# A two-layer mixer and mixture-of-experts backbone: the output projection in two parts, and expert products on tiles of 32 columns

## The chip, the cores and the metric

The kernel runs on one core of one Trainium2 chip. The time is the device time of one execution in microseconds. Before the change it is 1985.58 us in the median of three runs (1981.42 to 1986.17). One further execution was profiled: 1986.72 us, of which the profile's span, from the first instruction to the last, is 1984.9 us.

## The reference

Two layers run over 512 tokens of 1024 channels, 256 of context and 256 latent. Each layer normalises, projects to the inputs of four token mixers (latent attention, HGRN2, windowed attention with a sink, retention), concatenates their outputs, applies one output projection and adds it, gated, to the stream. Then comes a feed-forward part: dense SwiGLU in layer 0, eight SwiGLU experts of width 3584 with the best two per token in layer 1, where only the 256 latent tokens are still needed. Cut to what the change touches:

```python
h_lat = h_lat + g_a * (o_lat @ w_out[l])
if with_ctx:
    h_ctx = h_ctx + cg_a * (o_ctx @ w_out[l])
...
def swiglu(h, w_gate, w_up, w_down):
    return (jax.nn.silu(h @ w_gate) * (h @ w_up)) @ w_down
...
# layer 1: gates is zero for all but the two best experts of a token
h_lat = h_lat + g_f * sum(gates[..., e] * swiglu(a, w_gate[e], w_up[e], w_down[e]) for e in experts)
```

All of it is in 32-bit floats.

## The kernel before, in words

**The stream** is kept transposed, `hT`, as eight column tiles of 128 channels by 512 tokens. **The mixers** of a layer (`layer`) are written as generators: `s_win` (input projection), two `s_hgrn`, `s_attn`, `s_swa`, `s_ret` and `s_ada` (the modulation of later parts). `run_streams` (L276) draws from them in the order of an estimated clock: a generator yields the time that its step is thought to take, or the name of an event that it waits for, and `fire` sets an event. The framework's scheduler then orders the instructions of each engine, with what comes first in the program first where both are ready; `issue_after` (L450, L1192) only keeps loads behind a given load on the queue of SyncE (SP).

**The output projection** is `resid` (L1136) with an order of its rows, called when all mixers are written out: for each of eight column tiles m it loads 128 columns of `w_out` in four pieces, splits them into a rounded and a remainder part (`wsplit`, L253), multiplies all eight row tiles k by three products each (`mm3k`, L268, line L274 in the profile), adds the gated result to `hT` (L1159) and squares the tile for the next norm. The rows stand in the order 2, 3 (HGRN2), 0, 1 (latent attention), 6, 7 (retention), 4, 5 (windowed attention). Two PSUM banks (`mmt`) hold the sums. In layer 1 only columns 256 to 512 are computed, and after each tile `scaled` (L1286) feeds the router.

**The experts.** Tokens are ranked per expert; up to 128 go through `expert_steps` (L1482) in two shares of 64 slots. TensorE holds tokens as weights and streams the expert's weights past them. The first share uses two column tiles of 64 side by side, each with half of the columns. The second share runs by the number of tokens n, read into a register of TensorE: not at all for n <= 64, on four column tiles of 32 with a quarter of the columns each for n <= 96 ("quarters"), or on two tiles of 64 ("halves"). `rest_of` (L1461) is that branch (profile lines L1471 and L1472); it holds the last step of the first share, too, once in each arm. The width of 3584 is cut into stretches of 1024, 1024, 1024 and 512. A piece is one load of 2 MB: four steps k of 128 rows for gate and up (eight in the last stretch) and for down. One expert is 21 pieces. `prods` (L1487, products at L1496) and `d_step` (L1537, products at L1556) multiply a piece; `act_t` (L1522) transposes the activations of both shares between pieces, always; `scatter` (L1634) brings an expert's rows back to their tokens, one expert later. `load` (L1443) puts the pieces into eight buffers in turn, on SP's queue, each when TensorE has done with the buffer's last piece.

The products of the first share, before:

```python
for i in range(parts):       # parts = 2, m = 64
    last["pe"] = PE.matmul(dst[m * i:m * i + m, 0:c], x[k][:, 0:m], w(k)[:, c * i:c * i + c], start=(start and k == 0),
                           stop=(stop and k == nk - 1), tile_position=(0, m * i))
```

Of the kernel before, what the change touches and what calls it, by code (L numbers as in the profile page):

```python
# [9 lines left out]
F32 = mybir.dt.float32  # L10
# [131 lines left out]
def kernel(  # L142
# [88 lines left out]
    last = {}  # L231
# [284 lines left out]
    def layer(l):  # L516
# [111 lines left out]
        def s_win():  # L628
            ps_ = [mmt(), mmt(), pst("s")]
            mm3k([p[:, (0 if items[n][2] else q0):512] for n, p in enumerate(ps_)], first,  # L630
                 lambda k, n: tuple(u[k][:, (0 if items[n][2] else q0):512] for u in a), 8)
            if l == 0:
                with tc.issue_after(last["ada"].ins):
                    SP.dma_start(cs1, consts[:, nper:nall])
            ws = {NF: prep(items[NF], l == 0)}
            for n in range(NF):
                items[n][3](ps_[n])
                yield 5.2
                if items[n][4]:
                    fire(items[n][4])  # L640
            for n in range(NF, len(items)):
                kind, c0, full, fn, e = items[n]
                if n == 10:
                    with tc.issue_after(last["w"].ins):
                        load_small()
                if n + 1 < len(items):
                    ws[n + 1] = prep(items[n + 1])
                if l == 0 and F1 and n == len(items) - EA:
                    ada_ahead(range(1), F1[0])
                w = ws.pop(n)  # L650
                if kind == "t":
                    for j in range(4):
                        p = mmt()
                        ts = slice(j * 128, j * 128 + 128)
                        seq = [(k, 0, 0) for k in range(8)] + [(k, 1, 0) for k in range(8)] + [(k, 0, 1) for k in range(8)]
                        for i, (k, x_, y_) in enumerate(seq):
                            PE.matmul(p[:, 0:256], a[x_][k][:, ts], w[k // 4][y_][:, k % 4, :], start=(i == 0), stop=(i == 23))
                        fn(j, p)
                        yield 2.6
                else:  # L660
                    p = mmt() if n > NF else pst("s")
                    s0 = 0 if full else q0
                    mm3(p[:, s0:512], w, aview(a, s0, 512), 8)
                    fn(p)
                    yield 5.2 if s0 == 0 else 2.6
                if e:
                    fire(e)


        def seg(t, hs, c0=0):  # L670
# [446 lines left out]

        def s_ada():
            a = range(4, 12) if l == 0 else range(NF1 + G1, 12)
            for n0 in range(0, len(a), 4):  # L1120
                yield from ada_steps(l, a[n0:n0 + 4], AP[l], WM if l == 0 else "rrrr")

        run_streams([(0.0, s_win()), (0.0, s_hgrn(0)), (0.0, s_hgrn(1)), (0.0, s_attn()), (0.0, s_swa()),
                     (0.0, s_ret()), (AS[l], s_ada())], ev, clock)


        order = (2, 3, 0, 1, 6, 7, 4, 5)
        if l == 0:
            if F1[1:]:
                ada_ahead(range(1, len(F1)), F1[1:])  # L1130
            if F1:
                ada_fill()
            ada_ahead(range(len(F1), len(F1) + len(F2)), F2)
        return lambda after=None: resid(l, 2, w_out[l], lambda k, t=0: osp[order[k]], 8, q0, order=order, after=after)

    def resid(l, gi, w, a, nk, q0, k0=0, order=None, last=True, after=None):  # L1136
        def prep(m):
            if order is None:
                return wsplit(wload([(w, m * 128, 128)], nk=nk, k0=k0))
            raw = rawt([128, nk, 128])  # L1140
            for i in range(0, nk, 2):
                SP.dma_start(raw[:, i:i + 2, :], w[order[i] * 128:order[i] * 128 + 256, m * 128:(m + 1) * 128]
                             .rearrange("(k p) f -> p k f", p=128))
            return wsplit(raw)

        nxt = prep(0)
        for m in range(8):
            w2 = nxt
            if m < 7:
                nxt = prep(m + 1)  # L1150
            p = mmt()
            if order is None:
                mm3(p[:, q0:512], w2, a, nk)
            else:
                mm3k([p[:, q0:512]], [w2], a, nk)
            for i, (c0, c1) in enumerate(((256, 512), (0, 256))):
                if c0 < q0:
                    continue
                V.scalar_tensor_tensor(hT[:, m, c0:c1], p[:, c0:c1], modT[l][:, 8 * gi + m, i:i + 1],  # L1159
                                       hT[:, m, c0:c1], op0=ALU.mult, op1=ALU.add)  # L1160
            for m2 in (m - 1, m) if m == 7 else (m - 1,) if m else ():
                if last:
                    norm_sq(m2, q0, 512)
                if after:
                    after(m2)

    def head_stat(sq, q0):

# [225 lines left out]
    y_t = pgu.tile([128, 2, 512], F32, name="y")  # L1394
    for t in (*gu_t, y_t):
        V.memset(t[:, 1], 0.0)
    ptr = ctx.enter_context(tc.tile_pool(name="ptr", bufs=2, space=PSUM, reuse_waits="tile"))


    def acc(j, hf=None):  # L1400
# [8 lines left out]
        return p.rearrange("p (a b) -> p a b", b=256)  # L1409

    def ptile(name):
        return ptr.tile([128, 512], F32, tag="tr", name=name)

    def gather(P):

# [66 lines left out]
    def expert_steps(e, xT, done, n_e=None):  # L1482
# [4 lines left out]
        def prods(p, xA, xB, w, start, stop):  # L1487

            nk = len(xA)
            n = w(0).shape[-1]  # L1490

            def part(dst, x, parts, ks=range(nk)):
                m, c = 128 // parts, n // parts
                for k in ks:
                    for i in range(parts):
                        last["pe"] = PE.matmul(dst[m * i:m * i + m, 0:c], x[k][:, 0:m], w(k)[:, c * i:c * i + c], start=(start and k == 0),  # L1496
                                               stop=(stop and k == nk - 1), tile_position=(0, m * i))

# [23 lines left out]
        def act_t(m):  # L1522

            nb = STRETCH[m][1] // 256
            ps = [ptile("actA"), ptile("actB")]

            def tr(b, n):
                for i in range(n):
                    PE.transpose(ps[b][:, i * 128:(i + 1) * 128], at[m][:, b, i * 128:(i + 1) * 128], ident)  # L1529

            tr(0, nb)
            tr(1, nb)
            acts[m] = mt.tile([128, 2, 512], F32, tag="act", name="act", bufs=2)
            S.copy(acts[m][:, 0, 0:128 * nb], ps[0][:, 0:128 * nb])  # L1534
            V.tensor_copy(acts[m][:, 1, 0:128 * nb], ps[1][:, 0:128 * nb])  # L1535

        def d_step(m, f0):  # L1537
            def use(raw):
                if m == 0 and f0 == 0:
                    y.append(y_t)  # L1540
                nf = STRETCH[m][1] // 128
                b = acts[m]
                end = m == 3

                def act(part, parts):

                    w = 128 // parts
                    per = nf // parts
                    return [b[:, part, f % per * 128 + f // per * w:f % per * 128 + f // per * w + w] for f in range(f0, f0 + 4)]

                def part(i, parts, ks=range(4)):
                    w, c = 128 // parts, 1024 // parts
                    x = act(i, parts)
                    for k in ks:
                        for j in range(parts):
                            last["pe"] = PE.matmul(y[0][w * j:w * j + w, i, 0:c], x[k], raw[:, k, c * j:c * j + c],  # L1556
                                                   start=(m == 0 and f0 == 0 and k == 0), stop=(end and k == 3), tile_position=(0, w * j))
# [76 lines left out]
    def scatter(ys, PT, gate, n_e=None):  # L1634
        t, tq_ = PT
        for j in range(2):
# [139 lines left out]
```

## Time and profile before

| | us |
|---|---|
| median of three runs | 1985.58 |
| lowest, highest | 1981.42, 1986.17 |
| the profiled execution | 1986.72 |
| its span, first to last instruction | 1984.9 |
| in it, TensorE busy with products | 1883.2 |
| in it, from the first expert's product to the last one's | about 891 (1076 to 1967) |

In the rows further on, PE is TensorE's products, PEld its weight loads, DVE VectorE, ACT ScalarE, POOL GpSimd, and an engine's name with q is its sequencer or queue (PEldq: branches of TensorE's program). L12 is line 12 of the kernel. A number in brackets behind x counts instructions. In a timeline, neighbouring instructions of a kind are merged, and a bracket at the end tells how long the engine was idle before it and what ended that. E0 to E7 are the eight experts in the order in which they run.

### The profile page before, as it was taken

To read this page: it belongs to the slowest core of one execution; us is meant where nothing else is said; L and a number is where in the kernel's file an instruction comes from. 1 tells how busy PE (TensorE), PEld (TensorE's weight loads), DVE (VectorE), ACT (ScalarE), POOL (GpSimd) and SP (SyncE) were. 2 spreads that over 40 slices of the span, in tenths; PEclk is the share of its full clock that TensorE was granted. 3 is DMA by queue.
4 is the path that set the end of the run, shared out by engine and by line. 5 is a ranking of instruction groups with operands and counts; after the bars stand their busy time and mean duration, and the time that the engine had idled before them with its cause. 6 is when DMAs were issued, how large, how long until landed. Compare 5 with 4: busy or idle time off the path is not lost. (4 is left out here: it accounts for less than half of the span.)

```text
span 1984.9 us, 29168 instructions
## 1 busy us (share of the span) xinstructions
PE 1883.2 (95%) x12351; PEld 1120.6 (56%) x12351; DVE 683.7 (34%) x1333; ACT 430.5 (22%) x747; POOL 200.2 (10%) x245
## 2 busy tenths in 40 slices
PE   5999999999999999999988999999999999799996
PEld 3767754667888888787565453434435343334432
DVE  5874545353333334785533011111011112111022
ACT  3332434242223233434331100000000000000010
POOL 0442131110000000452320000000000000000000
PEclk9998998999999999999978999999999999999998
DMA  9334423525533343332455889999999999999995
GB/s 317 92 107 127 129 96 107 171 64 180 138 96 96 96 128 106 84 86 96 153 200 205 335 335 392 403 408 403 392 344 340 395 403 407 404 408 395 408 398 206
DMA packets 262353, 478.66 MB, mean 241 GB/s; under 512 B 16144, under 2 KB 142096, under 8 KB 262032
## 3 DMA queue, kind: packets, MB, share of 16 engines
q1 hardware_dynamic: 262160, 475.76, 66.0%
q8 instruction: 161, 2.64, 0.5%
q14 instruction: 32, 0.26, 0.0%
HBM read 474.68 MB, written 1.05 MB: 240 GB/s over the span
## 5 line engine op out<-in xcount | busy, mean ns | idle before, releaser
L1496 PE MATMUL u<-raw,xT 128*64 128x512 f32 (+3 forms) x2048 | 261.5, 452 | 14.2 <-issue 6.4
L1556 PE MATMUL y<-raw,act 128*64 128x512 f32 (+1 forms) x1792 | 260.6, 492 | 9.3 <-issue 6.5
L1496 PE MATMUL g<-raw,xT 128*64 128x512 f32 (+3 forms) x2048 | 258.3, 449 | 4.9 <-DMA raw<-in_moe_w_gate_dram 4.9
L256 ACT CAST wh<-raw 128x1024 fp32r<-128x1024 f32 (+1 forms) x129 | 132.8, 1038 | 326.4 <-PE mm L266 173.0
L257 DVE TENSOR_TENSOR wl<-raw,wh 128x1024 fp32r<-128x1024 f32 (+1 forms) x129 | 159.5, 1242 | 115.4 <-ACT wh L256 90.4
L1496 PEld LDWEIGHTS u<-raw,xT 128*64 128x64 f32 (+1 forms) x2048 | 101.0, 124 | 167.5 <-issue 137.2
L1496 PEld LDWEIGHTS g<-raw,xT 128*64 128x64 f32 (+1 forms) x2048 | 100.6, 123 | 151.4 <-issue 127.1
L1556 PEld LDWEIGHTS y<-raw,act 128*64 128x64 f32 (+1 forms) x1792 | 88.1, 124 | 159.0 <-issue 141.5
L1518 DVE TENSOR_TENSOR at<-at,u 128x1024 f32<-128x1024 f32 (+1 forms) x32 | 34.7, 1085 | 267.8 <-PE u L1496 267.8
L266 PE MATMUL mm<-ah,wh 128*128 128x512 f32 (+1 forms) x400 | 101.2, 388 | 0.0
L266 PE MATMUL mm<-al,wh 128*128 128x512 f32 (+1 forms) x400 | 96.0, 377 | 0.0
L1534 ACT COPY act<-actA 128x512 f32<-128x512 f32 (+1 forms) x32 | 17.0, 532 | 351.4 <-PE actA L1529 351.4
L266 PE MATMUL mm<-ah,wl 128*128 128x512 f32 (+1 forms) x400 | 93.0, 373 | 0.0
L1744 POOL TENSOR_TENSOR rs<-ss,mhalf 128x1 f32<-128x1 f32 x2 | 1.1, 564 | 908.6 <-DVE ss L1743 908.6
L266 PEld LDWEIGHTS mm<-ah,wh 128*128 128x128 f32 x400 | 70.3, 191 | 20.1 <-issue 6.2
L266 PEld LDWEIGHTS mm<-al,wh 128*128 128x128 f32 x400 | 71.0, 189 | 13.8 <-issue 0.8
L266 PEld LDWEIGHTS mm<-ah,wl 128*128 128x128 f32 x400 | 70.5, 188 | 12.8
L1516 ACT ACTIVATE at<-g 128x1024 f32<-128x1024 f32 (+1 forms) x32 | 29.3, 917 | 207.9 <-PE g L1496 207.9
L1535 DVE COPY act<-actB 128x512 f32<-128x512 f32 (+1 forms) x32 | 20.0, 625 | 153.1 <-PE actB L1529 153.1
L1159 DVE SCALAR_TENSOR_TENSOR hT<-mm,mod,hT 128x256 f32<-128x256 f32 x72 | 31.8, 480 | 96.9 <-PE mm L266 69.1
L371 POOL TENSOR_TENSOR rs<-ms,mhalf 128x4 f32<-128x4 f32 (+1 forms) x8 | 8.8, 1103 | 476.8 <-DVE ms L369 476.8
L1666 DVE TENSOR_TENSOR hT<-sc,hT 128x512 f32<-128x512 f32 x32 | 22.0, 688 | 92.2 <-PE sc L1648 53.4
(424 smaller groups left out, 2585.4 us busy)
## 6 DMA issues: line engine op xcount, KB each, us to landing
raw<-in_moe_w_gate_dram SPq DMA_DIRECT2D x56, 2048.0 KB, 21.2
raw<-in_moe_w_up_dram SPq DMA_DIRECT2D x56, 2048.0 KB, 21.0
raw<-in_moe_w_down_dram SPq DMA_DIRECT2D x56, 2048.0 KB, 19.9
raw<-in_w_ada_dram SPq DMA_DIRECT2D x64, 512.0 KB, 4.8
raw<-in_w_in_dram SPq DMA_DIRECT2D x44, 512.0 KB, 3.8
raw<-in_ffn_w_gate_dram SPq DMA_DIRECT2D x22, 512.0 KB, 3.8
raw<-in_ffn_w_up_dram SPq DMA_DIRECT2D x22, 512.0 KB, 3.9
adaw<-in_w_ada_dram SPq DMA_DIRECT2D x10, 1024.0 KB, 7.9
```

The costliest lines, as they stand in the source:

```text
L256: S.copy(wh, raw)
L257: V.tensor_tensor(wl, raw, wh, op=ALU.subtract)
L266: PE.matmul(p, uk, a(k)[hl], start=(n == 0), stop=(n == len(seq) - 1))
L371: G.tensor_tensor(r[:, j0:j1], ms[:, j0:j1], mhalf[:, j0:j1], op=ALU.pow)
L1159: V.scalar_tensor_tensor(hT[:, m, c0:c1], p[:, c0:c1], modT[l][:, 8 * gi + m, i:i + 1], hT[:, m, c0:c1], op0=ALU.mult, op1=ALU.add)
L1496: last["pe"] = PE.matmul(dst[m * i:m * i + m, 0:c], x[k][:, 0:m], w(k)[:, c * i:c * i + c], start=(start and k == 0), stop=(stop and k == ...
L1516: S.activation(at[m][:, :, 0:width], ps[0][:, :, 0:width], AF.Silu)
L1518: V.tensor_tensor(at[m][:, :, 0:width], at[m][:, :, 0:width], ps[1][:, :, 0:width], op=ALU.mult)
L1534: S.copy(acts[m][:, 0, 0:128 * nb], ps[0][:, 0:128 * nb])
L1535: V.tensor_copy(acts[m][:, 1, 0:128 * nb], ps[1][:, 0:128 * nb])
L1556: last["pe"] = PE.matmul(y[0][w * j:w * j + w, i, 0:c], x[k], raw[:, k, c * j:c * j + c], start=(m == 0 and f0 == 0 and k == 0), stop=(end ...
L1666: V.tensor_tensor(z, by2(ps[h]), res(h), op=ALU.mult)
```

## The change

The output projection becomes two generator-like parts of four row tiles each (`wo_part`). Part 0, rows of HGRN2 and latent attention, is a further stream, `s_wo`, which waits for the events of the input projection, the gate's modulation, both HGRN2 halves and the end of latent attention. Part 1, retention and windowed attention, runs where the whole projection ran. Each part loads 256 columns at a time and adds its sum to `hT`, so each tile is accumulated twice. In `act_t` the last transpose of the first share and those of the second go into `rest_of`: none of the second share for n <= 64, half of them for n <= 96. The scatter's quarters are contracted over 64 rows on two row tiles, not over 128. All products of experts use four column tiles of 32; where the share has 64 rows, two tiles get the same columns of the weights. Four fixed PSUM tiles replace a pool of two for transposes and the like.

```diff
+        def s_wo():
+            for e in ("win", "gate", "hgrn0", "hgrn1", "mla_done"):
+                yield e
+            yield from wo_part(0)
+
+        def wo_part(part, after=None):
+            rows = ((2, 3, 0, 1), (6, 7, 4, 5))[part]
+            def prep(m):
+                raw = rawt([128, 4, 256])
+                for i in (0, 2):
+                    last["w"] = SP.dma_start(raw[:, i:i + 2, :], w_out[l][rows[i] * 128:rows[i] * 128 + 256, m * 128:m * 128 + 256]
+                                             .rearrange("(k p) f -> p k f", p=128))
+                return wsplit(raw)
+            nxt = prep(0)
+            for m in range(8):
+                if m % 2 == 0:
+                    w2 = nxt
+                    if m < 6:
+                        nxt = prep(m + 2)
+                p = mmt()
+                f = slice(m % 2 * 128, m % 2 * 128 + 128)
+                mm3k([p[:, q0:512]], [[u[:, :, f] for u in w2]], lambda k, t: osp[rows[k]], 4)
...
-        order = (2, 3, 0, 1, 6, 7, 4, 5)
...
-        return lambda after=None: resid(l, 2, w_out[l], lambda k, t=0: osp[order[k]], 8, q0, order=order, after=after)
...
                 for k in ks:
-                    for i in range(parts):
-                        last["pe"] = PE.matmul(dst[m * i:m * i + m, 0:c], x[k][:, 0:m], w(k)[:, c * i:c * i + c], start=(start and k == 0),
-                                               stop=(stop and k == nk - 1), tile_position=(0, m * i))
+                    for i in range(4):
+                        s0, c0 = i * 32 % m, i * 32 // m * c
+                        last["pe"] = PE.matmul(dst[32 * i:32 * i + 32, 0:c], x[k][:, s0:s0 + 32], w(k)[:, c0:c0 + c],
+                                               start=(start and k == 0), stop=(stop and k == nk - 1), tile_position=(0, 32 * i))
...
-            tr(0, nb)
-            tr(1, nb)
+            tr(0, nb - 1)
+            def fin():
+                PE.transpose(ps[0][:, (nb - 1) * 128:nb * 128], at[m][:, 0, (nb - 1) * 128:nb * 128], ident)
+            rest_of(n_e, fin, lambda: tr(1, nb // 2), lambda: tr(1, nb))
...
-                for q in range(4):
-                    PE.matmul(ps[q // 2][:, q % 2 * 256:q % 2 * 256 + 256], tq_[:, q, js], ys[:, 1, 0:256], start=False, stop=(q % 2 == 1))
+                for i in range(2):
+                    for h in range(2):
+                        r = slice(64 * h, 64 * h + 64)
+                        PE.matmul(ps[h][:, i * 256:i * 256 + 256], tq_[r, 2 * h + i, js], ys[r, 1, 0:256], start=False, stop=(i == 1),
+                                  tile_position=(64 * h, 0))
```

`d_step` is changed as `prods` is.

## Rows read from the trace of the kernel before

**Rows 1.** Busy time by stretch, E0 to E7: us, engines (instructions), clock, DMA share, GB/s.

```profile
1076.00:1207.00 131.00, 131.00 (x1200) 57.76 (x1200) 12.02 (x23) 12.05 (x18) 0.00 (x0) 1.00 0.84 317
1207.00:1300.00 93.00, 88.92 (x458) 36.41 (x456) 17.34 (x29) 7.55 (x11) 0.00 (x0) 0.98 1.03 403
1300.00:1425.00 125.00, 125.00 (x1180) 53.44 (x1176) 17.34 (x29) 7.55 (x11) 0.00 (x0) 1.00 1.03 402
1425.00:1553.00 128.00, 128.00 (x1188) 56.09 (x1188) 17.34 (x29) 7.55 (x11) 0.00 (x0) 1.00 0.94 351
1553.00:1647.00 94.00, 88.78 (x468) 36.75 (x462) 17.34 (x29) 7.55 (x11) 0.00 (x0) 1.00 1.03 404
1647.00:1747.00 100.00, 86.95 (x440) 33.77 (x438) 17.34 (x29) 7.55 (x11) 0.00 (x0) 0.98 1.03 405
1747.00:1874.00 127.00, 125.83 (x1182) 53.74 (x1180) 16.99 (x28) 7.72 (x12) 0.00 (x0) 1.00 1.02 403
1874.00:1968.00 94.00, 87.97 (x441) 35.48 (x438) 14.94 (x22) 8.54 (x13) 0.00 (x0) 0.98 0.91 358
```

**Rows 2.** Waits in 1090:1985, longest of SP's queue and of TensorE: us, times, longest.

```profile
SPq L1453 <- PE u L1496: 242.4, 50, 15.1
...
PE y L1556 <- issue: 6.5, 3, 2.8
```

**Rows 3.** Straight code, 500.4:785.5: busy time, and packets of the instruction queue.

```profile
500.40:785.50 285.10, 285.10 (x1261) 235.72 (x1260) 103.59 (x138) 77.83 (x92) 0.00 (x0) 1.00 0.37 108
...
q8 instruction: 10, 0.16, 0.2%
```

**Rows 4.** Instruction queue in E2 (1300:1425) and E4 (1553:1647): packets, MB, share.

```profile
q8 instruction: 14, 0.23, 0.7%
...
q8 instruction: 14, 0.23, 1.0%
```

**Rows 5.** One source line: branches in E1, and the last jump: ns min/median/max, starts.

```profile
L1471 PEldq COMPARE_BRANCH  x20: 208/426/5622, 1208.9 to 1295.4; - x20
...
L1714 PEldq COMPARE_BRANCH  x1: 3750/3750/3750, 1971.8 to 1971.8; - x1
```

**Rows 6.** Timeline of TensorE in E1: start, us, instruction, idle time before it.

```profile
1290.50 1.98 PE L1556 MATMUL y<-raw,act 128*64 128x512 f32 x4 [2.64 <-issue]
```

**Rows 7.** Instruction queue in 1924:1953 (E7) and in 1148.9:1154.1 (E0).

```profile
q8 instruction: 5, 0.08, 1.2%
...
q8 instruction: 2, 0.03, 2.5%
```

**Rows 8.** Timeline: two pieces of a heavy expert, two of a light one.

```profile
1336.28 10.97 PE L1496 MATMUL u<-raw,xT 128*64 128x512 f32 x96
...
1671.70 7.04 PE L1496 MATMUL u<-raw,xT 128*64 128x512 f32 x32
```

**Rows 9.** Busy time inside one second share, on tiles of 32 columns.

```profile
1322.73:1324.03 1.30, 1.30 (x28) 0.78 (x24) 0.00 (x0) 0.00 (x0) 0.00 (x0) 1.00 1.03 413
```

**Rows 10.** Timeline: transposes of the second share, and one scatter's quarters.

```profile
1330.30 0.60 PE L1529 MATMUL actB<-cs,at 128*128 128x128 f32 x4
...
1215.19 1.99 PE L1648 MATMUL sc<-ys,PTq 128*128 128x256 f32 x8
```

**Rows 11.** Layer 0: one of three product groups in 358:410, and a stretch before.

```profile
L274 PE MATMUL mm<-oh,wh 128*128 128x512 f32 x54 | 21.9, 412 | 2.6 <-ACT oh L824 2.0 <-DVE hT L1159 0.6
...
310.00:320.00 10.00, 10.00 (x32) 4.53 (x30) 5.09 (x13) 4.21 (x7) 0.00 (x0) 0.54 0.65 179
```

**Rows 12.** Layer 1: product groups in 1024.4:1062, and a stretch before.

```profile
L274 PE MATMUL mm<-o,wh 128*128 128x256 f32 x108 | 22.3, 307 | 0.0
L274 PE MATMUL mm<-o,wl 128*128 128x256 f32 x54 | 16.2, 299 | 0.0
...
1010.00:1020.00 10.00, 9.08 (x26) 3.63 (x26) 2.87 (x9) 0.37 (x1) 0.42 (x1) 0.52 0.09 12
```

**Rows 13.** The page's costliest groups: accumulation into the stream, busy us, mean ns, idle.

```profile
L1159 DVE SCALAR_TENSOR_TENSOR hT<-mm,mod,hT 128x256 f32<-128x256 f32 x72 | 31.8, 480 | 96.9 <-PE mm L266 69.1
```

More of the change, by code (lines that the diff above doesn't have):

```diff
@@ L667, in s_win @@
                     fire(e)
+            fire("win")
         def seg(t, hs, c0=0):
@@ L1119, in s_ada @@
             a = range(4, 12) if l == 0 else range(NF1 + G1, 12)
+            if l:
+                fire("gate")
             for n0 in range(0, len(a), 4):
                 yield from ada_steps(l, a[n0:n0 + 4], AP[l], WM if l == 0 else "rrrr")
+                if l == 0 and n0 == 0:
+                    fire("gate")
+        def s_wo():
[19 more added lines that the diff above has]
+                mm3k([p[:, q0:512]], [[u[:, :, f] for u in w2]], lambda k, t: osp[rows[k]], 4)
+                for i, (c0, c1) in enumerate(((256, 512), (0, 256))):
+                    if c0 < q0:
+                        continue
+                    V.scalar_tensor_tensor(hT[:, m, c0:c1], p[:, c0:c1], modT[l][:, 16 + m, i:i + 1],
+                                           hT[:, m, c0:c1], op0=ALU.mult, op1=ALU.add)
+                if part == 1:
+                    for m2 in (m - 1, m) if m == 7 else (m - 1,) if m else ():
+                        norm_sq(m2, q0, 512)
+                        if after:
+                            after(m2)
+                yield 2.8 if WC else 1.5
         run_streams([(0.0, s_win()), (0.0, s_hgrn(0)), (0.0, s_hgrn(1)), (0.0, s_attn()), (0.0, s_swa()),
-                     (0.0, s_ret()), (AS[l], s_ada())], ev, clock)
-        order = (2, 3, 0, 1, 6, 7, 4, 5)
+                     (0.0, s_ret()), (AS[l], s_ada()), (0.0, s_wo())], ev, clock)
         if l == 0:
@@ L1133, in layer, with last_part, resid @@
             ada_ahead(range(len(F1), len(F1) + len(F2)), F2)
-        return lambda after=None: resid(l, 2, w_out[l], lambda k, t=0: osp[order[k]], 8, q0, order=order, after=after)
-    def resid(l, gi, w, a, nk, q0, k0=0, order=None, last=True, after=None):
-        def prep(m):
[L1138 to L1144, printed above, removed]
+        def last_part(after=None):
+            for _ in wo_part(1, after):
+                pass
+        return last_part
+    def resid(l, gi, w, a, nk, q0, k0=0, last=True):
+        def prep(m):
+            return wsplit(wload([(w, m * 128, 128)], nk=nk, k0=k0))
         nxt = prep(0)
@@ L1151, in resid @@
             p = mmt()
[L1152 to L1155, printed above, removed]
+            mm3(p[:, q0:512], w2, a, nk)
             for i, (c0, c1) in enumerate(((256, 512), (0, 256))):
-                if c0 < q0:
-                    continue
                 V.scalar_tensor_tensor(hT[:, m, c0:c1], p[:, c0:c1], modT[l][:, 8 * gi + m, i:i + 1],
@@ L1163, in resid @@
                     norm_sq(m2, q0, 512)
-                if after:
-                    after(m2)
     def head_stat(sq, q0):
@@ L1396 @@
         V.memset(t[:, 1], 0.0)
-    ptr = ctx.enter_context(tc.tile_pool(name="ptr", bufs=2, space=PSUM, reuse_waits="tile"))
+    tr_t = [pgu.tile([128, 512], F32, name="tr"[:i + 1]) for i in range(2)]
+    for t in tr_t:
+        V.memset(t, 0.0)
+    ntr = [0]
     def acc(j, hf=None):
@@ L1411, in ptile @@
     def ptile(name):
-        return ptr.tile([128, 512], F32, tag="tr", name=name)
+        ntr[0] += 1
+        return tr_t[ntr[0] % 2]
     def gather(P):
@@ L1554, in part @@
                     for k in ks:
-                        for j in range(parts):
-                            last["pe"] = PE.matmul(y[0][w * j:w * j + w, i, 0:c], x[k], raw[:, k, c * j:c * j + c],
-                                                   start=(m == 0 and f0 == 0 and k == 0), stop=(end and k == 3), tile_position=(0, w * j))
+                        for j in range(4):
+                            s0, c0 = j * 32 % w, j * 32 // w * c
+                            last["pe"] = PE.matmul(y[0][32 * j:32 * j + 32, i, 0:c], x[k][:, s0:s0 + 32], raw[:, k, c0:c0 + c],
+                                                   start=(m == 0 and f0 == 0 and k == 0), stop=(end and k == 3), tile_position=(0, 32 * j))
                 part(0, 2, range(3))
```

## The prediction

> **What bounds the kernel now.** I read the busy time of the engines per expert first [rows 1]. The eight experts take 891 of the 1984.9 us of span, and they are of two kinds. In E0, E2, E3 and E6, 1180 to 1200 matmuls run and TensorE is busy from end to end for 125 to 131 us; in E1, E4, E5 and E7 some 440 to 470 run, in 93 to 100 us, with 4 to 13 us of idle time. So the first four have between 65 and 96 tokens (both shares, the second in the layout of quarters) and the others at most 64. The DMA column of the same rows says what else is near its limit: E1, E2, E4, E5 and E6 move 402 to 405 GB/s, which no longer stretch exceeds, while E0 has 317 and E3 351. An expert's weights are 21 pieces of 2.097 MB, at 405 GB/s 108.7 us. Experts with two shares are slower than that on TensorE, the others faster, and eight buffers carry the difference from one to the next. The waits of the DMA queue agree: its loads wait for TensorE to hand a buffer back, 242 us for one line alone, and TensorE shows little idle time of its own, the largest piece of it "issue", with no releaser [rows 2].
>
> A third limit shows only in that word. The queue of kind "instruction" brings TensorE's code in packets of 16.4 KB. In 285 us of straight code, ten came while 1261 matmuls and 1260 weight loads ran [rows 3]: 252 instructions a packet. An expert takes 14 packets whether it runs both shares or one [rows 4], so the branches that it skips are fetched all the same. In E1, a light expert right behind a heavy one, the branch at L1471, 0.208 us at its shortest, has a median of 0.426 and once took 5.62 us [rows 5], and TensorE then idles 2.64 us on "issue" [rows 6]: some 3 us of products were queued, the rest of the wait is lost. With the DMA engines full, packets that are wanted at once come every 5.8 us: five in 29 us [rows 7]. At 317 GB/s two came within 5.2 us, and the jump at the end, with the DMA idle, waited 3.75 us for its target [rows 5, 7]. So code is had ahead by little more than one packet, and its price depends on how full the DMA is. Before the change that is enough: 14.2 packets x 5.8 = 82 us, less than any expert.
>
> **The change, part by part.**
>
> *Tiles of 32 columns.* Two pieces of a heavy expert take 10.97 us, two of a light one 7.04 [rows 8]: 5.485 and 3.52 each, so the second share costs 1.965 us a piece. On its own ground it runs six groups of four matmuls in 1.30 us [rows 9], 0.215 a group, and has eight groups: 1.72. The other 0.245 us goes where the array changes from 64-column tiles to 32 and back. With one width it should go; 0 to 0.29 are the bounds, and I take 0.245, since nothing else differs at that place. Over 21 pieces x 4 experts: -20.6 us. Four 512-column streams side by side cost what two did if they run as the four 256-column ones do now; I take that at no cost, hidden by the same concurrency.
>
> What it adds is code. A product of the first share had two matmuls on two tiles, each executed as two passes with their weight loads: 8 instructions per step k. On four tiles it has 16. The last k stands in three branches, and the "halves" branch (never run here) doubles too. A piece of four steps goes from 24 + 3x8 + 32 + 64 = 144 instructions to 48 + 3x16 + 64 + 64 = 224; one of eight steps (two per expert, the last 512 columns of gate and up) from 272 to 416. Per expert 19 x 80 + 2 x 144 = 1808, with the branched transposes 1860, or 7.3 packets: 14.1 becomes 21.4.
>
> *Transposes in the branch.* Heavy: the second share's four become two, from 0.60 us [rows 10], in three stretches, and one of two in the fourth: -0.9 each, -3.5 in all. Light: -2 us each, but there they hide behind code or DMA; zero, and without that cover -8 for all four.
>
> *Scatter two row tiles wide.* Its eight matmuls took 1.99 us [rows 10], twice per heavy expert. Side by side in pairs, as the first share's already are, about half: -1.9 us per heavy expert. It runs within the next expert, which is heavy only for E2. So -1.9; the other three (-5.7) hide like the transposes.
>
> *Output projection.* Before, the products of both halves stand after the mixers, but for the first half of two column tiles that PSUM had room for. Six tiles x 12 products can move ahead. Layer 0: 54 of each of three kinds run in 358:410 [rows 11], 162 in 52 us, of which some 14 go to other products and idle time: 0.23 each, 16.4 us of work. Layer 1: 108 and 54 run in 1024.4:1062 [rows 12], where other groups hold half of the 37.6 us: 0.12 each, 8.6 us. Cover for it: the stretches before, where the clock falls to half, 0.54 at 310:320 and 0.52 at 1010:1020, because TensorE waits there [rows 11, 12]. Against it: 16 accumulations more in layer 0 and 8 in layer 1, 0.48 us each [rows 13], 11.5 us on a VectorE that the softmax chain also uses, and products that stand ahead of that chain on TensorE's queue. Bounds: +5 (chain delayed, nothing hidden) and -27 (16.4 + 8.6 and 2 us for a warmer clock). I take -9 and -7, -16 in all. The queue of SP issues half as many loads of twice the size; the first expert load now stands behind the last w_out load instead of the last w_in load, but seven of the eight did so in time already. Taken at zero; up to 3 us if the first piece lands late.
>
> **The new bound.** Where the DMA is full, 21.4 packets x 5.8 = 124 us is more than 108.7. Then TensorE falls behind, buffers stay full, the DMA gets pauses, and packets come faster. With 5.2 us at 317 GB/s and 5.8 at 405, an expert of T us moves 44.04 MB/T: at T = 115, 383 GB/s, between the two, 5.65 by a straight line, which gives 121 us; by the 3.75 us of idle DMA as the other end, weighted with the DMA's idle share, 5.7. Throttled loads also come one or two at a time instead of four in a queue, as in E0, which speaks for less. I take 5.35 and T = 114.5; the ends are 108.7 (DMA pace) and 124. E1, E4 and E5 go from 93, 94 and 100 to 114.5: +21.5, +20.5, +14.5. In E7 loads end some six pieces before the work, so those run at 3.52 us: about 10 us less, 104.5 instead of 94, +10.5. Sum +67. In heavy experts a normal piece (230 instructions with branches, 4.8 us of fetch) hides behind 5.24 us of products; the two eight-step pieces, 422 instructions, need 8.6 us each against 5.24, less some 2 us for what TensorE has queued, an estimate from rows 5 and 6 with products of half the length: +4.7 per expert, +19.
>
> **Sum**, against the profiled run (span 1984.9, 1986.7 with what lies around it): -16 (projection) -20.6 -3.5 -1.9 (heavy experts) +19 (their code) +67 (light experts) = +44, so 2030.6. The profiled run is 1.1 above the median of 1985.6; the prediction for the median is 2029.
>
> By the Trainium skill (Runtime: NRT & Kernel Launch, Instruction fetch mechanics) TensorE's instruction memory holds 2048 instructions, refilled in blocks of 256 as a FIFO. By that, eight blocks of stock from E0 would carry E1, and the time would be that of the first rival; the branches of E1, directly behind a heavy expert, speak against it [rows 5]. The same section says that a taken branch out of the two-page window waits for a fetch, as rows 5 and 6 show.
>
> **Rivals.** (A) Code is not the limit: packets come faster when more are wanted, and 5.8 us was the pace of demand. For it: E4 wanted a packet only every 6.7 us on average (14 in 94 us [rows 4]). Against: the even spacing where they are wanted at once, and the idle "issue". Then the heavy experts' gain counts where the DMA had room, E0 and E2 with E3: about -20, light ones stay at DMA pace, front -16: 1950, faster. It decides if packets can come every 5.1 us (108.7 / 21.4) on a full DMA. (B) Fetching stays at 5.8 us throughout: light +31, +30, +24 and E7 +20 = +105; heavy eight-step pieces 9.6 us, +27, which eats the 26 gained: 1986.7 + 105 + 1 - 16 = 2077. (C) The gap between shares is the branch's and not the width's: the 20.6 us stay, 2051. (D) Part one of the projection delays the mixers: +5 instead of -16, 2051.
>
> **How the numbers follow.** Forecast 0.53 (its own range 1995 to 2060), A 0.18, B 0.13, C 0.08, D 0.08. The range of 8 in 10 leaves out most of A and the top of B: 1972 to 2080. What a measurement here tells from no change is 0.3%, 6 us. Faster is A and little else: 0.19; within 0.3%: 0.05; slower: 0.76.
>
> **What would show it.** In the profile after: some 21 code packets per expert; L1471 branches in light experts with a median over 1 us and "issue" as the main idle time of TensorE there; light experts of 110 to 124 us at under 395 GB/s; heavy pieces of 5.2 to 5.25 us except the eight-step ones; w_out products starting before 300 and layer 1's first expert product some 15 us earlier. If light experts stay below 101 us, the code argument is wrong and the kernel is faster.

## The result, and the profile after

The changed kernel takes 2057.92 us, the median of four runs (2047.13 to 2062.85). Four runs of the kernel before, on the same chip, have a median of 1983.5. The ratio is 1.037, with a 95% interval of 1.032 to 1.042: slower. The forecast was 2029, in a range of 1972 to 2080.

The profiled execution is the quickest of the four, 2047.13 us with a span of 2045.3. Against the span before, that is 60.4 us more, and it is these 60.4 that the trace can account for; between the medians there are 74. What makes the other runs of the changed kernel longer, 10.8 us in the median, stays open.

First the busy time by stretch, E0 to E7, with the columns of [rows 1].

```profile
1053.50:1182.50 129.00, 125.04 (x1566) 59.95 (x1569) 12.02 (x23) 12.16 (x18) 0.00 (x0) 0.99 0.86 322
1182.50:1302.70 120.20, 96.70 (x814) 32.83 (x810) 16.97 (x29) 7.55 (x11) 0.00 (x0) 0.91 0.95 360
1302.70:1429.00 126.30, 120.66 (x1541) 54.46 (x1537) 16.97 (x29) 7.55 (x11) 0.00 (x0) 1.00 0.95 361
1429.00:1557.10 128.10, 122.61 (x1557) 55.55 (x1553) 16.97 (x29) 7.59 (x12) 0.00 (x0) 0.99 0.92 347
1557.10:1675.70 118.60, 94.52 (x814) 32.61 (x810) 16.98 (x29) 7.51 (x11) 0.00 (x0) 0.96 0.95 363
1675.70:1798.30 122.60, 92.54 (x798) 29.15 (x794) 16.97 (x29) 7.59 (x12) 0.00 (x0) 0.96 0.97 371
1798.30:1923.80 125.50, 120.92 (x1541) 53.67 (x1537) 16.62 (x28) 7.56 (x12) 0.00 (x0) 0.99 0.94 356
1923.80:2028.50 104.70, 88.43 (x794) 28.70 (x786) 14.43 (x21) 8.12 (x13) 0.00 (x0) 0.98 0.76 291
```

The heavy experts (E0, E2, E3, E6) have hardly changed. The light ones have gone from 93 to 100 us to 119 to 123 (E7 to 105), though TensorE has 92 to 97 us of work in the longer three, and the DMA, full before at 402 to 405 GB/s, now moves 360 to 371. Neither is at its limit, so a third thing is. The waits of TensorE from 1055 to 2030 (us, times, longest) point to it: "issue" is time in which an engine waits for nothing that the profile shows. It compares with 6.5 us in three waits for the largest line of before [rows 2]:

```profile
PE u L1534 <- issue: 51.4, 29, 4.1
PE g L1534 <- issue: 43.6, 29, 4.0
PE y L1599 <- issue: 15.5, 13, 3.5
```

The instruction queue on the page, then in E1 and E2 (packets, MB, share of 16 engines):

```profile
q8 instruction: 219, 3.59, 0.7%
...
q8 instruction: 22, 0.36, 1.2%
...
q8 instruction: 21, 0.34, 1.0%
```

In place of 14 packets [rows 4] an expert now takes 20 to 22. Last, where the projection ends in layer 0 and in layer 1: the accumulations of the output projection into the stream, on VectorE (start, us). The first three lines are the changed kernel, the first of them an early one of part 0; the last two are the last of each layer in the kernel before.

```profile
285.95 0.88 DVE L1156 SCALAR_TENSOR_TENSOR hT<-mm,mod,hT 128x256 f32<-128x256 f32 x2 [0.95 <-PE mm L274]
388.12 0.88 DVE L1156 SCALAR_TENSOR_TENSOR hT<-mm,mod,hT 128x256 f32<-128x256 f32 x2 [0.34 <-PE mm L274]
1036.00 0.48 DVE L1156 SCALAR_TENSOR_TENSOR hT<-mm,mod,hT 128x256 f32<-128x256 f32 x1 [0.87 <-PE mm L274]
```

```profile
409.65 0.88 DVE L1159 SCALAR_TENSOR_TENSOR hT<-mm,mod,hT 128x256 f32<-128x256 f32 x2 [2.71 <-PE mm L274]
1060.02 0.48 DVE L1159 SCALAR_TENSOR_TENSOR hT<-mm,mod,hT 128x256 f32<-128x256 f32 x1 [2.31 <-PE mm L274]
```

It ends 21.5 us earlier in layer 0, 24.0 us in layer 1, and the first expert product starts at 1053.5 instead of 1075.9. From there, by the ends of the experts (to a tenth of a microsecond, when ScalarE copies the expert's result), the difference of the spans is made up so:

| us | before | after | difference |
|---|---|---|---|
| up to the first expert product | 1075.9 | 1053.5 | -22.4 |
| heavy experts, four | 131.3 + 124.5 + 128.5 + 126.1 | 129.0 + 126.3 + 128.1 + 125.5 | -1.5 |
| light experts, four | 93.5 + 93.5 + 100.5 + 93.4 | 120.2 + 118.6 + 122.6 + 104.7 | +85.2 |
| the rest | 17.7 | 16.8 | -0.9 |
| span | 1984.9 | 2045.3 | +60.4 |

### The profile page after: what moved, and what is told of

Read it like the earlier page. It is cut to its first block, busy times and chain, and to the rows that moved or that the text cites. A ratio compares the mean times of both kernels' runs of the same rounds, so it can differ in the third digit from the quotient of the medians.

```text
span 2045.3 us, 34899 instructions
## 1 busy us (share of the span) xinstructions
PE 1860.2 (91%) x15211; PEld 1092.0 (53%) x15211; DVE 689.8 (34%) x1359; ACT 431.1 (21%) x747; POOL 202.1 (10%) x245
## 5 line engine op out<-in xcount | busy, mean ns | idle before, releaser
L1534 PE MATMUL u<-raw,xT 128*32 128x512 f32 (+2 forms) x3072 | 274.2, 497 | 51.5 <-issue 51.4
L1534 PE MATMUL g<-raw,xT 128*32 128x512 f32 (+2 forms) x3072 | 266.0, 480 | 43.6 <-issue 43.6
L1599 PE MATMUL y<-raw,act 128*32 128x512 f32 (+1 forms) x2688 | 264.1, 533 | 15.6 <-issue 15.5
L1534 PEld LDWEIGHTS u<-raw,xT 128*32 128x32 f32 x3072 | 102.0, 115 | 214.5 <-issue 191.8
L1534 PEld LDWEIGHTS g<-raw,xT 128*32 128x32 f32 x3072 | 97.4, 110 | 196.5 <-issue 171.4
L1599 PEld LDWEIGHTS y<-raw,act 128*32 128x32 f32 x2688 | 88.6, 111 | 166.4 <-issue 147.2
L1576 ACT COPY act<-t 128x512 f32<-128x512 f32 (+1 forms) x16 | 8.5, 533 | 203.9 <-PE t L1572 105.0
L1576 ACT COPY act<-tr 128x512 f32<-128x512 f32 (+1 forms) x16 | 8.5, 532 | 198.9 <-PE t L1567 105.3
L266 PE MATMUL s<-ah,wh 128*128 128x512 f32 x192 | 47.6, 390 | 0.0
L266 PE MATMUL s<-al,wh 128*128 128x512 f32 x192 | 47.4, 389 | 0.0
```

The lines of the kernel that those rows point to most:

```text
L266: PE.matmul(p, uk, a(k)[hl], start=(n == 0), stop=(n == len(seq) - 1))
L1534: last["pe"] = PE.matmul(dst[32 * i:32 * i + 32, 0:c], x[k][:, s0:s0 + 32], w(k)[:, c0:c0 + c], start=(start and k == 0), stop=(stop and k ...
L1599: last["pe"] = PE.matmul(y[0][32 * j:32 * j + 32, i, 0:c], x[k][:, s0:s0 + 32], raw[:, k, c0:c0 + c], start=(m == 0 and f0 == 0 and k == 0 ...
```

## The experiments

Theory 1 is that of the forecast: TensorE's code arrives in packets, whether it is executed or jumped over, and the light experts wait for it. Its main rival is that the narrow tiles themselves run slower. Ratios are against the kernel before, run on the same chip.

**The changed kernel with less code that is never run.**

```
-        with tc.If(n_e[0] > 64) as b1:
-            with tc.If(n_e[0] > 96) as b2:
-                halves_()
-            with b2.Else():
-                halves_(quarters)
+        with tc.If(n_e[0] > 64) as b1:
+            halves_(quarters)
```

> The changed kernel without the arm of the branch for over 96 tokens of an expert; no expert here has so many, so no product that is executed is left out, but the program is shorter: a normal expert piece has 144 TensorE instructions of code in place of 224, an eight-step piece 272 in place of 416, which is what the kernel before has. Theory 1 (the instruction packets of TensorE set the pace, and skipped code is fetched too): packets per expert fall from about 21 to about 14, light experts go back from 120 us to 93 to 96, heavy ones to 121 to 126, and the whole to 1935 to 1965 us. Rival (the narrower tiles themselves, four streams of 32 columns, are slow): light experts stay at 118 to 122 us and the whole at 2040 to 2060.

Measured: 1945.1 us, ratio 0.981 (0.977 to 0.984). E0, E1 and E2:

```profile
1058.20:1181.90 123.70, 123.43 (x1566) 59.67 (x1569) 12.01 (x23) 12.17 (x18) 0.00 (x0) 1.00 0.89 334
1181.90:1270.90 89.00, 85.72 (x814) 30.91 (x810) 16.98 (x29) 7.56 (x12) 0.00 (x0) 0.98 1.03 404
1270.90:1391.20 120.30, 119.54 (x1541) 53.52 (x1537) 16.97 (x29) 7.55 (x11) 0.00 (x0) 1.00 1.03 406
```

The same instructions are executed (x814 in E1 either way), and 14 packets come in E1 in place of 22. With that the light expert falls from 120.2 to 89.0 us and the DMA is full again. The whole falls by 113 us between the medians, 102.6 between the spans. The edit takes the inner branch away, too, but a light expert doesn't reach that one, so for light experts it removes the suspected cause alone, and the loss goes with it. The waits on "issue" go from 110.5 us in the three groups above to 10.3. The eight-step pieces of E2 show the same in a heavy expert. First the changed kernel (start, us, instruction, idle time before it), then this run:

```profile
1396.80 3.21 PE L1534 MATMUL g<-raw,xT 128*32 128x256 f32 x56
1400.19 2.39 PE L1534 MATMUL g<-raw,xT 128*32 128x256 f32 x72 [0.18 <-issue]
...
1406.38 2.37 PE L1534 MATMUL u<-raw,xT 128*32 128x256 f32 x54 [1.66 <-issue]
1411.60 1.17 PE L1534 MATMUL u<-raw,xT 128*32 128x128 f32 x34 [2.85 <-issue]
```

```profile
1363.06 5.38 PE L1531 MATMUL g<-raw,xT 128*32 128x256 f32 x128
1368.66 5.18 PE L1531 MATMUL u<-raw,xT 128*32 128x256 f32 x119 [0.22 <-issue]
1374.34 0.49 PE L1531 MATMUL u<-raw,xT 128*32 128x128 f32 x9 [0.49 <-issue]
```

The two pieces take 16.0 us (1396.80 to 1412.77) with the long code and 11.8 (1363.06 to 1374.83) with the short: 4.2 us, where 4.7 were forecast.

**The wider tiles again, all else as changed.**

```
-                    for i in range(4):
-                        s0, c0 = i * 32 % m, i * 32 // m * c
...
+                    for i in range(parts):
+                        last["pe"] = PE.matmul(dst[m * i:m * i + m, 0:c], x[k][:, 0:m], w(k)[:, c * i:c * i + c], ...)
```

(and the same in the down products)

> The changed kernel with the expert products of the first share on tiles of 64 columns again, as before; the output projection in two parts, the branch around the transposes and the new scatter stay. Theory 1 (code, by way of the tile width): experts as before, light ones 93 to 95 us, about 14 packets each, and the whole at 1952 to 1962 us (before less 22 for the projection, less some 5 for transposes and scatter). Rival (the new branch around the transposes is what costs, by a taken jump more per stretch): light experts stay above 105 us, the whole above 2000.

Measured: 1959.68 us, ratio 0.986 (0.984 to 0.989). E1 takes 89.1 us with 14 packets, so the branch around the transposes isn't what costs. This version keeps all three arms and is faster than both kernels. Two pieces of a heavy expert, here and in the changed kernel, which has the same branches:

```profile
1347.96 10.97 PE L1533 MATMUL u<-raw,xT 128*64 128x512 f32 x96
```

```profile
1371.31 10.50 PE L1534 MATMUL u<-raw,xT 128*32 128x512 f32 x128
```

The narrow tiles do save about what was forecast of them, 0.235 us a piece for 0.245. In whole experts, at about the same code, E0, E2, E3 and E6 take 129.8, 124.5, 125.5 and 126.1 us here, 123.7, 120.3, 121.6 and 123.9 in the run with one arm less: 16.4 in all (there the inner branch is gone as well; what that does is told with the last runs).

**The kernel before with more code that is never run.**

```
-lambda: part(p[:, 1], xB, 2))
+lambda: (part(p[:, 1], xB, 2, (0, 1)), part(p[:, 1], xB, 2), part(p[:, 1], xB, 2)))
```

(in the last place of the branch, the arm for over 96 tokens; the same in the down products)

> The kernel before with code that is never executed: the arm for over 96 tokens has its products two and a half times over, so that a piece has 224 instructions of TensorE code (416 in an eight-step piece), as the changed kernel has; no expert here takes that arm. Executed instructions, tile widths and transfers are those of before. Theory 1: light experts slow from 93.5 us to 117 to 121, the last to about 104, heavy ones by 2 to 6 us each, and the whole goes to 2065 to 2095 us. Rival (tile width, not code): nothing changes, 1978 to 1990.

Measured: 2029.95 us, ratio 1.021 (1.018 to 1.024), under the 2065 to 2095 of theory 1. The edit had been counted wrongly: the arm has 12 matmuls more in four steps, not 20, so a piece has 144 + 12 x 4 = 192 instructions and an eight-step piece 352. Theory 1 then wants 19 x 48 + 2 x 80 = 1072 more instructions per expert, 4.2 packets, 18.3 in all. E1, and its packets:

```profile
1210.80:1315.70 104.90, 92.39 (x458) 37.73 (x458) 17.35 (x29) 7.60 (x12) 0.00 (x0) 0.98 1.03 404
```

```profile
q8 instruction: 17, 0.28, 1.1%
```

On the page the queue has 194 packets against 161: 33 more in eight experts, 4.1 each. Not one executed instruction differs from the kernel before (x458 matmuls in E1, as in [rows 1]), and the light expert is 11.4 us slower. So the tile width isn't needed for the loss; code that is only jumped over makes it.

**The changed kernel with its unused arm on wide tiles**, which gives it the same 192 instructions:

```
-lambda: part(p[:, 1], xB, 2))
+lambda: part(p[:, 1], xB, 2, wide=True))      # wide: tiles of m columns, as before
```

> The changed kernel with only the arm for over 96 tokens (not executed here) back on tiles of 64 columns; all else, and all that is executed, is the changed kernel's. A normal piece has 192 instructions of code, an eight-step piece 352, what the run of the kernel before with more code had (its arm came out at 192, not at the 224 meant). Theory 1: about 18 packets per expert, light experts 102 to 107 us as in that run, the whole 1985 to 2005. Rival (tiles cost by themselves): light experts at 115 or more, the whole over 2035.

Measured: 2002.82 us in two runs, ratio 1.010 (1.007 to 1.014).

```profile
1195.00:1300.50 105.50, 88.40 (x810) 32.47 (x802) 16.97 (x29) 7.51 (x11) 0.00 (x0) 0.98 1.03 405
```

```profile
q8 instruction: 18, 0.29, 1.1%
```

At equal code the light experts are equal to 0.6 to 2.2 us: E1, E4, E5 and E7 take 105.5, 106.1, 112.1 and 96.1 us on narrow tiles, 104.9, 104.7, 109.9 and 95.1 on wide ones in the run above. (The narrow version has the branched transposes besides, some 50 instructions an expert.) That settles between theory 1 and the tile width.

**The unused arm twice, and eight times.** The first edit is in the changed kernel, the second in the kernel before:

```
-lambda: part(p[:, 1], xB, 2))
+lambda: (part(p[:, 1], xB, 2), part(p[:, 1], xB, 2)))
```

```
-lambda: part(p[:, 1], xB, 2))
+lambda: [part(p[:, 1], xB, 2) for _ in range(8)])
```

> The changed kernel with the products of the arm for over 96 tokens (not executed here) standing twice: 288 instructions of code in a normal piece, 544 in an eight-step one, about 27 packets per expert; executed work is the changed kernel's. If a packet has one price of 5.7 us, every expert, heavy or light, takes 152 to 158 us and the whole goes to 2270 to 2320. If the price falls because the weight transfers leave the DMA engines idle for longer, light experts take 115 to 140 us, heavy ones 130 to 140, and the whole 2080 to 2180.

> The kernel before with its never executed arm for over 96 tokens eight times over: 368 instructions of code in a normal piece, 720 in an eight-step one, and a light expert's jump skips 336 and more of them, over a whole packet of 256. If skipped code is fetched whatever its length: 34 packets per expert, 150 us and more for each, the whole over 2400. If only blocks that execution enters (and perhaps the next one) are fetched: 22 to 28 packets per expert, and light experts at 105 to 145 us.

Measured: 2230.91 us in two runs (ratio 1.126, 1.121 to 1.130) and 2375.79 us in one run. E1 and its packets in the first, E5 and its packets in the second:

```profile
1205.50:1344.70 139.20, 102.72 (x814) 32.77 (x810) 17.00 (x29) 7.59 (x12) 0.00 (x0) 0.89 0.85 319
...
q8 instruction: 27, 0.44, 1.2%
```

```profile
1897.70:2041.70 144.00, 101.28 (x442) 35.96 (x440) 17.34 (x29) 7.55 (x12) 0.00 (x0) 0.91 0.83 307
...
q8 instruction: 32, 0.52, 1.7%
```

A packet has no one price: 139.2 / 27 is 5.2 us, 144.0 / 32 is 4.5. The first total lies between the two expectations: above the 2080 to 2180 of a falling price, since the heavy experts took 148 to 152 us in place of 130 to 140, and below the 2270 to 2320 of one price. The second total came out below 2400 although nearly all the code was fetched (30 to 35 packets per expert, where 34 were counted): a jump over 336 instructions, more than a packet holds, saved little of the fetching (30 to 33 packets in the light experts).

**The projection alone.** The kernel before with only the output projection in two parts.

> The kernel before with the output projection in two parts alone; the expert section is that of before. Theory: the first expert product starts about 22 us earlier and the experts keep their times, 1955 to 1966 us. Rival (the earlier projection takes from the mixers or from the first expert's loads what it gives): above 1972.

Measured: 1967.12 us, ratio 0.989 (0.985 to 0.993). The last accumulation of either layer, and the first expert product:

```profile
394.20 0.88 DVE L1156 SCALAR_TENSOR_TENSOR hT<-mm,mod,hT 128x256 f32<-128x256 f32 x2 [0.34 <-PE mm L274]
1047.53 0.48 DVE L1156 SCALAR_TENSOR_TENSOR hT<-mm,mod,hT 128x256 f32<-128x256 f32 x1 [0.87 <-PE mm L274]
1062.87 5.52 PE L1528 MATMUL g<-raw,xT 128*64 128x512 f32 x48
```

In this execution the first expert product is 13 us earlier, and the experts take 889.6 us against 891.3 before, so the gain stays whole. The median lies just above the 1966 that was expected and below the 1972 of the rival; the four runs spread from 1959 to 1973. Over the nine kernels here that have the new projection, the first expert product starts between 1053.5 and 1065.0, 1059.1 on average; in the three without it, between 1075.9 and 1078.6, 1077.3 on average: some 18 us.

**Three ways to keep the narrow tiles with less code.** All put the unused arm on wide tiles and have the last step of the first share fewer times than three: in the two outer arms, once ahead of the branch, or once behind it.

```
+        with tc.If(n_e[0] > 64) as b1:      # "in": 176 instructions a piece
+            last_a()
+            with tc.If(n_e[0] > 96) as b2:
+                halves()
+            with b2.Else():
+                quarters()
+        with b1.Else():
+            last_a()
```

> As the run above, but the last step of the first share stays inside the branch, once in the outer taken arm ahead of the inner branch and once in the other arm: 176 instructions for a normal piece, 336 for an eight-step one, both branches kept. Theory 1: about 17 packets per expert, light experts 92 to 98 us, heavy ones 121 to 125, the whole 1945 to 1970. If the narrow tiles save nothing by themselves and the shorter heavy experts of the run with one arm less came from the inner branch that went, the heavy ones are at 124 to 130 here.

> The changed kernel with less code for the same executed work: the last step of the first share stands once, ahead of the branch, in place of three times in its arms, and the arm for over 96 tokens (not executed here) is on tiles of 64 columns; everything executed stays on tiles of 32. A normal expert piece has 160 TensorE instructions of code, an eight-step piece 320 (changed kernel 224 and 416, before 144 and 272). Theory 1 (code): about 16 packets per expert, light experts 89 to 95 us, heavy ones 120 to 124, the whole 1940 to 1960 us. Rival (the branch needs the last step inside its arms as cover): each of the 21 pieces loses 0.3 to 1 us more, light experts 96 to 110, the whole 1970 to 2050.

> As the run with the last step ahead of the branch (160 instructions in a normal piece, 320 in an eight-step one, the arm for over 96 tokens on 64 columns and not executed here), but with the last step once behind the branch, so that the branch stands where it stands in the kernel before, with queued products ahead of it. If the 102 us of the light experts there came from waits for the branch: no such waits here, about 15.6 packets of 5.9 us, light experts 90 to 96 us, heavy ones 120 to 124, the whole 1945 to 1960. If they came from the packets all the same: 99 to 103 us again, the whole 1965 to 1980.

Measured: 1968.07 us inside (ratio 0.993, 0.990 to 0.995), 1980.56 ahead (0.999, 0.997 to 1.001), 1980.0 behind (0.998, 0.995 to 1.001). E1 with the step inside, then with it behind, and TensorE's waits in 1190:1290 of that run:

```profile
1185.70:1286.80 101.10, 89.45 (x814) 32.46 (x810) 16.97 (x29) 7.54 (x11) 0.00 (x0) 0.97 1.03 406
```

```profile
1186.60:1286.80 100.20, 90.38 (x814) 32.58 (x810) 17.10 (x29) 7.55 (x11) 0.00 (x0) 1.00 1.02 401
...
PE y L1596 <- PEq L1503: 2.9, 7, 0.6
...
PE g L1530 <- PEq L1503: 1.3, 5, 0.6
PE u L1530 <- PEq L1503: 1.2, 7, 0.2
```

With 17 packets the light expert takes 101 us, 5.9 each: as theory 1 has it, though above the 92 to 98 that its text gave. With 15 or 16, and the step outside, E1, E4 and E5 take 99 to 103, where 89 to 96 were expected: the packets alone don't explain that. With the last step outside the arms, on either side, TensorE waits for the branch (L1503) again and again, 19 times and 5.4 us in the three groups shown; inside the arms, E1 has no such wait. So the copies of the last step are a cover for the branch, and taking them out gives back what the shorter code brings. The run with the step behind gives the 99 to 103 us that its text had for packets as the cause, but it was to be free of these waits and isn't, so it doesn't separate the two. Whether the rest of the excess is the branch too stays open.

With the step inside and both branches in place, the heavy E0, E2, E3 and E6 take 129.5, 122.6, 120.9 and 121.2 us. E2, E3 and E6 are as short as in the run with one arm less, or within 2.3 us of it, so there the narrow tiles save by themselves, without the inner branch going. E0 isn't: its 123.7 us were seen only with the shortest code, and here it waits 3.8 us on "issue".

## Why the prediction was right in kind and short in size

*Direction and cause: right.* The light experts lose by code packets: shown by taking the code away (E1 from 120.2 to 89.0 us), by adding it to the kernel before (93.5 to 104.9), and by equal times at equal code on both tile widths. Rival A, that packets come faster when more are wanted, falls: on a full DMA (399 to 406 GB/s) they came every 5.9 to 6.0 us on average (E1, E4 and E5 together: 51 in 304.3 us with the last step inside, 53 in 319.5 in the kernel before with more code, 55 in 323.7 with the unused arm wide), and none of the 150 intervals between two starts of packets in one expert is under 5.6. Rival C, the gap being the branch's, falls too: a pair of pieces goes from 10.97 to 10.50 us with both branches in place. Rival D falls by the projection alone.

*Packets per expert: right.* 21.4 counted, 20 to 22 seen; on the page 219 in place of 161, 7.25 more per expert for 7.3.

*The price of a packet: the term that was too small.* The straight line between 5.2 us at 317 GB/s and 5.8 at 405 gave 5.65 us and 121 us per expert; the prediction went below it, to 5.35 and 114.5, because throttled loads come one or two at a time. Measured, E1, E4 and E5 take 361.4 us for 64 packets: 5.65 each, 120.5 us on average, at 360 to 371 GB/s. The step down from the line had no row of its own behind it, and it cost 18 us, more than the 16.4 by which the whole sum missed the profiled execution (the heavy experts added 5.5, the projection and the rest took 7.3 off): +85.2 for the light experts in place of +67 (E1 +26.7 for +21.5, E4 +25.1 for +20.5, E5 +22.1 for +14.5, E7 +11.3 for +10.5). Rival B, 5.8 throughout, with 2077, lies 19 us from the median and the forecast 29; from the profiled execution they are 30 and 18 off. The truth was between them, and that it agrees with the line is in part luck: the line was read at 383 GB/s, and at the 360 to 371 that came it gives 5.5 to 5.6. What the trace shows isn't a line but two prices. Of the 61 intervals between starts of packets within E1, E4 and E5, 56 are 4.6 us or longer, 5.8 in the median, as on a full DMA, and five are 3.2 to 3.7 us, where the weight loads pause. In E1 two are that short, from 1276.3 and from 1292.3, and they meet the slices of 49 and 27 GB/s (slices of 3.0 us from 1182.5):

```profile
GB/s 398 412 304 403 383 410 354 390 372 390 395 384 384 312 393 380 397 401 390 385 394 404 409 405 413 406 412 360 418 356 403 184 49 368 344 398 254 27 337 409
```

So the loads that came one or two at a time didn't make a packet cheaper until they stopped for a while.

*Heavy experts.* Forecast -20.6 - 3.5 - 1.9 + 19 = -7, measured -1.5. The code came out as forecast in sum: 508.9 us with the long code, 489.5 with the arm and its branch removed, 19.4 (5.3, 6.0, 6.5 and 1.6). The gain under it was 20.9 instead of 26 (510.4 to 489.5): 4.5 from transposes and scatter, where 5.4 were forecast, and 16.4 from the narrow tiles, where 20.6 were. The saving per piece was right; it counted least in E6, 2.2 us, and most in E0, 6.1, which is the one with room on the DMA, 334 GB/s against 404 in E6. In rival A the prediction had said that the gain counts where the DMA has room, and then had not put it in its own sum. That this is the cause isn't shown: E2 gained 4.2 us at 406 GB/s and E3 3.9 at 392, and of E6's shortfall only 0.7 us are longer waits for weights (2.0 against 1.3). The scatter itself did what was said of it: its four pairs for a row tile run from 1189.63 to 1190.66 in the run with one arm less, 1.0 us for 1.99 [rows 10].

```profile
1189.63 0.38 PE L1690 MATMUL t<-ys,PTq 64*128 64x256 f32 x1
...
1190.28 0.38 PE L1690 MATMUL tr<-ys,PTq 64*128 64x256 f32 x1
```

*Output projection: right to the size that two executions can tell.* -16 forecast; -22.4 in the profile of the changed kernel, -13 alone, some -18 on average. The split over the layers was wrong: the gain is layer 0's, 21.5 and 15.5 us in the two profiles for the 9 forecast, and layer 1 adds 2.5 in one and loses 3.0 in the other, for 7. One row was misread: at half clock, 310:320, TensorE doesn't wait but is busy for all 10.00 us [rows 11]; it was idle in the 20 us before (8.26 and 7.30 us busy of 10).

*The signs that were named.* Right: packets, "issue" as the main idle time, light experts at 119 to 123 us under 395 GB/s, pieces of 5.25 us in heavy experts but for the eight-step ones, accumulations before 300; the first expert product came 22.4 us earlier, for some 15. Wrong: a branch median over 1 us in light experts. In E1 the branch of the changed kernel shows (ns min/median/max)

```profile
L1507 PEldq COMPARE_BRANCH  x26: 70/356/5445, 1182.3 to 1302.5; - x26
```

a median of 0.356. The wait for code stands ahead of the products, under "issue", and only now and then in the branch's own record.

By the Trainium skill (Runtime: NRT & Kernel Launch, Instruction fetch mechanics), TensorE's instruction memory is 2048 instructions, refilled in blocks of 256, which would be a stock of eight blocks; the section also says that the next page is fetched while the current one is executed. No stock of eight shows here: in E1, right behind a heavy expert, TensorE of the changed kernel is already idle 9 us in.

```profile
1191.14 1.19 PE L1534 MATMUL g<-raw,xT 128*32 128x512 f32 x8 [1.99 <-issue]
```

That heavy expert had waited for code itself, near its end. But in the run with one arm less E0 has no wait on "issue", and E1 still has 3.3 us of them, with 14 packets in 89.0 us.

## What to carry to other kernels

Count the code of a loop body that is written out, all arms of its branches included, and set packets times their price beside the other limits, as for any other transfer: an arm that never runs, with the branch to it, cost this kernel 113 us, and the price to take is the one measured where the DMA is full. Narrower tiles are worth their saving (0.235 us a piece here) only where code has room, and a copy of the last step in each arm is worth its code if it covers the branch. A line through two average prices can hide that there are only two prices: look at the single intervals before reading a lower one from it.

## What had not been expected of the hardware

The average price of a code packet falls with the load on the DMA, over a wide range. Light experts, E1, E4 and E5 together (in a single expert the count can be off by a packet, some 0.3 us of the price):

| kernel | packets | us | GB/s | us per packet |
|---|---|---|---|---|
| last step inside | 51 | 304.3 | 405 to 406 | 5.97 |
| unused arm wide | 55 | 323.7 | 399 to 405 | 5.89 |
| before, more code | 53 | 319.5 | 403 to 404 | 6.03 |
| changed | 64 | 361.4 | 360 to 371 | 5.65 |
| unused arm twice | 80 | 425.3 | 305 to 319 | 5.32 |
| unused arm eight times | 95 | 435.0 | 295 to 307 | 4.58 |
| changed, end of E7 | 10 | 34.0 | 7 | 3.4 |

Down to the fifth line the average falls because more packets meet a pause of the weight loads: intervals of 3.0 to 4.3 us are none of 150 in the first three kernels, 5 of 61 in the changed one and 16 of 77 with the arm twice, while the longer intervals keep a median of 5.8 to 5.9. The sixth line is of another kind: 12 of its 92 intervals are under 1.5 us, two packets all but at once, against one of 77 with the arm twice at about the same load. Only there does a light expert's jump in a four-step piece lead over more than a packet (336 instructions, 224 with the arm twice); that the pairs come from it isn't shown.

The last line is the stretch from 2003 to 2037, after the last weights have landed. Its busy time, and its packets:

```profile
2003.00:2037.00 34.00, 25.82 (x266) 9.26 (x258) 7.34 (x12) 2.74 (x6) 0.00 (x0) 0.92 0.02 7
```

```profile
q8 instruction: 10, 0.16, 2.0%
```

So with the DMA all but idle packets come every 3.4 us on average; TensorE is busy for 25.8 of the 34 us, so they aren't all wanted at once. And waiting for code goes with a lower clock: E1 has a granted clock of 0.91 on average in the changed kernel, where TensorE idles between pieces, and 0.98 with one arm less, where it stays busy; the same 814 matmuls are busy for 96.7 us in the one and 85.7 in the other.
